# Scaling on ScalarE, two rotary products and three heads turned by VectorE in the second layer of a hybrid encoder

## The chip, the cores and the metric

The kernel runs on one core of one Trainium2 chip. A core has five engines, each with a queue of its own that it works through in order: TensorE (PE in the profile, its weight loads PEld), VectorE (DVE), ScalarE (ACT), GpSimd (POOL) and SyncE (SP), which here only issues DMAs. They meet through semaphores. The metric is the device time of one execution in microseconds (us). Three runs of the kernel before gave 1989.08 us in the median, from 1989.07 to 1989.42.

## What is computed

A trunk of two layers on 256 tokens of width 2048, all in float32. Each layer runs 12 heads of a token mixer and 4 heads of cross-attention into 256 memory tokens, one output projection over all 16 heads, and a squared-ReLU MLP of width 8192. The second layer, the only one that the change touches, is this (cut from the reference):

```
z = n @ b_w_in[j]
q, k, v, qm = split(z, [1536, 2048, 2560])
q = axial_rope(rms_norm(split_heads(q, 12), b_q_norm[j]))
k = axial_rope(rms_norm(split_heads(k, 4),  b_k_norm[j]))
mix = gqa_block_attention(q, k, split_heads(v, 4))
        # per block: s = q k^T * scale; p = softmax(s); p @ v
cross = memory_attention(qm, km, vm)          # 4 heads
h = h + concatenate([mix, cross], -1) @ w_o[i]
# rotary: concatenate([x1*c - x2*s, x2*c + x1*s])
```

## The kernel before

**Products.** A float32 product is made of three fast ones: each operand is split into a rounded high part and the rest. `split` (L506 to L509) does this: ScalarE copies the source into the high part (L508), VectorE subtracts it (L509). Weights come from HBM by DMAs on SP's queue into one of three `raw` buffers (L274), are split in halves of 1024 columns into one of four `hi`/`lo` pairs, and are read by TensorE: twelve matmuls of 512 columns for a half, at L388 (high by high), L391 (high by low weights) and L392 (low by high weights).

**Order.** The Python program runs the halves ("grains") one after the other; each grain is a tick. Other steps are put in at a number of ticks later (`later`). The compiler's scheduler then fixes each engine's order, with this order as priority and a simulated time for readiness. `issue_after(x)` holds back those instructions of a block that run on the same engine as `x`; `past(fn, (a, v))` does so for an ScalarE and a VectorE instruction.

**Attention of the second layer.** The q heads come in three blocks of four (heads 0 to 3, 4 to 7, 8 to 11), each the product of 8 halves. `b_q_done` follows each: `normed_heads` makes the head norms (squares on ScalarE L1614, the root on GpSimd L517, the scaling L1620) and the rotary turn on VectorE: `o = y * cos` (L1600), four products of 32 columns for each head with the sines (L1606, 128x128 in all for each), and the sum (L1608). This is done for two tiles of 128 tokens. The queries are then turned so that a head's features lie on the partitions: block 0 by `queries_far`, block 1 by TensorE (`heads_T`), block 2 by `queries_aside`, where VectorE turns 32x32 blocks (L1582) and eight DMAs on GpSimd's queue (L1585) put them in place. `queries_aside` holds the turn back on VectorE until `box["pT", 5][1]`, the VectorE half of the split of head 5's probabilities.

`attention` gives each head four or three steps. Step 0, `attend`, makes scores on TensorE (L604 to L606), the negated row maximum on VectorE (L562), two exponentials with row sums on ScalarE (L564), the reciprocal of the sums (L567) and two multiplications by it (L569), both on VectorE; the result lies in a buffer `sc`, of which there are three. The last step, `attend3`, multiplies with the values (L698 to L700) and splits the head's output into `cat` (L508, L509), which the output projection reads. Between them the probabilities are turned, in one of two ways:

- three numbers in `steps`, such as `(0, 3, 6)`: `attend2` turns them with four TensorE operations (L616) into PSUM and splits that into `pT`;
- four numbers, such as `(0, 2, 5, 6)`: `turned` lets VectorE turn 32x32 blocks (two instructions, L668) into another of the three `sc` buffers, and four DMAs on SP's queue (L673) put them into the low half of `pT_t`; `halved` splits that in place.

The numbers are ticks after the head's first. Before, the first way is used for heads 4, 5, 6 and 8 to 11, the second for the memory heads and heads 0 to 3 and 7.

**After the last head.** The output projection's first two column blocks run beside all this. Their last chunk of weights, for heads 8 to 11, is handled by `late_products`, and its splits are held back behind certain steps: the first half of the second block behind `box["scaled", 9]`, the last scaling of head 9.

## Time and profile before

| | |
|---|---|
| median of three runs | 1989.08 us |
| the profiled execution, its own time | 1989.6 us |
| its span, first to last instruction | 1987.8 us |
| granted TensorE clock, mean | 0.999 |
| VectorE busy, whole span | 1729.1 us (87%) |
| ScalarE busy, whole span | 1443.7 us (73%) |
| second layer's memory heads, scores to outputs | about 1116 to 1157 us of the span |
| heads 0 to 11, scores to outputs | about 1193 to 1275 us of the span |

The page of the profile gives busy times of engines, the chain of work that ended last, and groups of instructions by line. The timeline gives start, duration, engine, line, operation, what is written from what, shape and count, and in brackets how long the engine stood idle before and for whom. A matmul's record lasts from its first row to the last of its result, so records overlap: what one costs TensorE is the distance from its start to the start of the next.

### The profile page before, as it was taken

The numbers are of one execution on the slowest core, as the hardware profiler recorded it, in microseconds if no ns is written. First come the engines' busy times: TensorE is split into PE (matmuls) and PEld (weight loads), VectorE is DVE, ScalarE is ACT, GpSimd is POOL, SyncE is SP. The second block draws the span as 40 slices with busy tenths as digits, with TensorE's granted clock in tenths as the row PEclk, the third lists the DMA queues.
The fourth block names the chain that finished last, engine by engine and source line by source line (L and its number), as shares of the span: only waits on it lengthen the run. The fifth ranks groups of instructions, "written<-read, shape, count | busy, mean of one in ns | idle before, by whom it ended". The sixth has DMA issues, their size and how long they took to land.

```text
span 1987.8 us, 33096 instructions
## 1 busy us (share of the span) xinstructions
PE 1977.8 (99%) x12816; PEld 1796.3 (90%) x12816; DVE 1729.1 (87%) x2098; ACT 1443.7 (73%) x2109; POOL 152.6 (8%) x205
## 2 busy tenths in 40 slices
PE   9999999999999999999999999999999999999998
PEld 8999999899999999999998888889999999999997
DVE  6777777589999999999999879789999999999997
ACT  6755555478887878777887657668788777877786
POOL 0000000000000000000001001001000000000001
PEclk9999999999999999999999999999999999999999
DMA  7856555768777777777778765668777777777775
GB/s 289 319 193 209 199 193 184 267 210 258 218 231 236 229 230 239 225 241 232 223 228 222 269 221 172 218 205 260 239 225 227 236 230 229 237 229 241 228 227 157
DMA packets 112862, 453.51 MB, mean 228 GB/s; under 512 B 19009, under 2 KB 42689, under 8 KB 65345
## 3 DMA queue, kind: packets, MB, share of 16 engines
q1 hardware_dynamic: 92320, 414.43, 61.1%
q0 software_dynamic: 20096, 36.45, 10.4%
q8 instruction: 100, 1.64, 0.3%
q10 hardware_dynamic: 288, 0.52, 0.1%
q14 instruction: 58, 0.47, 0.1%
HBM read 397.78 MB, written 4.19 MB: 202 GB/s over the span
## 4 chain that ended last, share of the span: by engine, by line
PE 98%; DVE 1%; issue 0%; DMA 0%; ACT 0%; SPq 0%; POOL 0%; DVEq 0%; POOLq 0%; ACTq 0%
PE ps_u L411 35%; PE ps_s L411 10%; PE p L1231 10%; PE p L1235 10%; PE p L1234 10%; PE ps_m L391 7%; PE ps_m L392 7%; PE ps_m L388 7%; DMA raw<-in_w_first 0%; PE sc_ps L605 0%; PE sc_ps L604 0%; PE sc_ps L606 0%; PE av L698 0%; PE av L699 0%; PE av L700 0%
## 5 line engine op out<-in xcount | busy, mean ns | idle before, releaser
L411 PE MATMUL ps_u<-hT,uh 128*128 128x256 f32 x3812 | 662.5, 276 | 0.0
L411 PEld LDWEIGHTS ps_u<-hT,uh 128*128 128x128 f32 x3812 | 578.7, 188 | 5.7
L411 PE MATMUL ps_u<-hT,ul 128*128 128x256 f32 x1964 | 542.6, 276 | 0.0
L508 ACT ACTIVATE uh<-raw_U 128x1024 fp32r<-128x1024 f32 x258 | 273.5, 1061 | 154.0 <-PE ps_u L411 151.6
L411 PEld LDWEIGHTS ps_u<-hT,ul 128*128 128x128 f32 x1964 | 368.7, 188 | 0.0
L508 ACT ACTIVATE hi<-raw 128x1024 fp32r<-128x1024 f32 (+1 forms) x215 | 222.1, 1037 | 183.0 <-PE ps_m L392 93.1
L509 DVE TENSOR_TENSOR lo<-raw,hi 128x1024 fp32r<-128x1024 f32 (+1 forms) x215 | 255.0, 1191 | 108.0 <-ACT hi L508 107.2
L509 DVE TENSOR_TENSOR ul<-raw_U,uh 128x1024 fp32r<-128x1024 f32 x258 | 314.2, 1219 | 9.2 <-ACT uh L508 9.2
L509 DVE TENSOR_TENSOR tl<-t,th 128x2048 fp32r<-128x2048 f32 x120 | 274.8, 2290 | 51.4 <-ACT th L508 51.1
L508 ACT ACTIVATE th<-t 128x2048 fp32r<-128x2048 f32 x120 | 231.0, 1925 | 91.3 <-PE p L1235 91.3
L509 DVE TENSOR_TENSOR bl<-b,bh 128x1536 fp32r<-128x1536 f32 x120 | 210.2, 1752 | 0.0
L1199 POOL DMA_DIRECT2D t<-b x120 | 104.4, 870 | 1156.9 <-ACT t L1198 1097.2
L1231 PE MATMUL p<-th,a_s 128*128 128x512 f32 x480 | 187.5, 391 | 0.0
L1234 PE MATMUL p<-tl,a_s 128*128 128x512 f32 x480 | 187.2, 390 | 0.0
L1235 PE MATMUL p<-th,a_s 128*128 128x512 f32 x480 | 186.7, 389 | 0.0
L508 ACT ACTIVATE bh<-b 128x1536 fp32r<-128x1536 f32 x120 | 178.8, 1490 | 3.5
L411 PE MATMUL ps_s<-nT,hi 128*128 128x256 f32 x896 | 154.6, 277 | 0.0
L1235 PE MATMUL p<-bh,a_s 128*128 128x512 f32 x360 | 140.9, 391 | 0.0
L1234 PE MATMUL p<-bl,a_s 128*128 128x512 f32 x360 | 140.1, 389 | 0.0
L1231 PE MATMUL p<-bh,a_s 128*128 128x512 f32 x360 | 140.1, 389 | 0.0
L411 PEld LDWEIGHTS ps_s<-nT,hi 128*128 128x128 f32 x896 | 135.3, 188 | 0.2
L411 PE MATMUL ps_s<-nT,lo 128*128 128x256 f32 x448 | 124.2, 277 | 0.0
(298 smaller groups left out, 3669.2 us busy)
## 6 DMA issues: line engine op xcount, KB each, us to landing
raw_U<-in_w_up SPq DMA_DIRECT2D x128, 1024.0 KB, 6.4
b<-in_w_pair SPq DMA_DIRECT2D x120, 1024.0 KB, 5.8
raw<-in_w_o SPq DMA_DIRECT2D x32, 1024.0 KB, 5.0
t<-b POOLq DMA_DIRECT2D x120, 256.0 KB, 6.6
raw<-in_w_b SPq DMA_DIRECT2D x21, 1024.0 KB, 5.4
raw<-in_w_av SPq DMA_DIRECT2D x12, 1024.0 KB, 5.0
raw<-in_w_aq SPq DMA_DIRECT2D x12, 1024.0 KB, 4.9
raw<-in_w_ak SPq DMA_DIRECT2D x12, 1024.0 KB, 4.8
```

What stands on the lines that cost most here:

```text
L388: first = nc.tensor.matmul(ps, ah, hi[:, s], start=st, stop=False)
L391: nc.tensor.matmul(ps, ah, lo[:, s], start=False, stop=False)
L392: final = nc.tensor.matmul(ps, al, hi[:, s], start=False, stop=sp)
L411: ins = nc.tensor.matmul(ps, x, acts[:, k, part], start=k == n == 0, stop=k == KT - 1 and n == 2)
L508: first = nc.scalar.activation(dst_hi, src, AF.Copy)
L509: return first, nc.vector.tensor_tensor(dst_lo, src, dst_hi.bitcast(F32), op=ALU.subtract)
L1199: nc.gpsimd.dma_start(s[:, 3, :], b[:, 1, :], accum_op=ALU.add)
L1231: ins = nc.tensor.matmul(ps, a[:, 0, ai, :], hi[:, s], start=entered, stop=False, skip_group_check=True)
L1234: nc.tensor.matmul(ps, a[:, 0, ai, :], lo[:, s], start=False, stop=False, skip_group_check=True)
L1235: nc.tensor.matmul(ps, a[:, 1, ai, :], hi[:, s], start=False, stop=ends, skip_group_check=True)
```

## The change

In the second layer (`box["layer"]` is 1 there) the two multiplications by the reciprocal go to ScalarE, for all 16 heads. The four sine products of the rotary turn become two, each over both halves of a head's features. And heads 4, 5 and 6 take the second way of turning; with head 7 they are now one call of `attention`, with the same first and last ticks as before.

```diff
@@ softmaxed
         for s in range(NT):
-            box["scaled"] = nc.vector.tensor_scalar(sc[:, s, :], sc[:, s, :], rs[:, s : s + 1], None, op0=ALU.mult)
+            if box["layer"]:
+                box["scaled"] = nc.scalar.activation(sc[:, s, :], sc[:, s, :], AF.Copy, scale=rs[:, s : s + 1])
+            else:
+                box["scaled"] = nc.vector.tensor_scalar(sc[:, s, :], sc[:, s, :], rs[:, s : s + 1], None, op0=ALU.mult)
@@ normed_heads, turned_by
-            for a in range(2):
-                for b in range(2):
-                    nc.vector.tensor_tensor(y2v[:, :, a, b, :], yv[:, :, a, 1 - b, :],
-                                            sv[:, None, a, b, :].to_broadcast([P, 4, 32]), op=ALU.mult)
+            for b in range(2):
+                nc.vector.tensor_tensor(y2v[:, :, :, b, :], yv[:, :, :, 1 - b, :],
+                                        sv[:, None, :, b, :].to_broadcast([P, 4, 2, 32]), op=ALU.mult)
@@ b_q_done
             if blk == 1:
-                attention(jobs[:3], 1, 2, (0, 3, 6))
-                attention(jobs[3:], 7, 2, (0, 2, 5, 6))
+                attention(jobs, 1, 2, (0, 2, 5, 6))
```

## The prediction

> **What bounds the kernel now.** I read the page of the profile first: its busy times, the row of granted clock, and the chain that ended last.

> ```profile
> PE 1977.8 (99%) x12816; PEld 1796.3 (90%) x12816; DVE 1729.1 (87%) x2098; ACT 1443.7 (73%) x2109; POOL 152.6 (8%) x205
> ...
> PEclk9999999999999999999999999999999999999999
> ...
> PE 98%; DVE 1%; issue 0%; DMA 0%; ACT 0%; SPq 0%; POOL 0%; DVEq 0%; POOLq 0%; ACTq 0%
> ```

> TensorE is busy for 1977.8 of 1987.8 us at full clock and carries 98% of the chain: only ten microseconds are not its own. So two things can move the time: fewer TensorE instructions, or a new hole between them. Second, the view of busy times by stretch, for the part in which heads 0 to 11 are worked on.

> ```profile
> core 0: us, PE busy (x) PEld busy (x) DVE busy (x) ACT busy (x) POOL busy (x), PEclk, DMA share, GB/s
> 1190.00:1230.00 40.00, 40.00 (x205) 34.23 (x204) 34.46 (x68) 29.46 (x88) 7.03 (x8) 1.00 0.53 181
> 1230.00:1250.00 20.00, 20.00 (x113) 17.30 (x112) 18.88 (x38) 11.91 (x27) 4.48 (x8) 1.00 0.66 201
> 1250.00:1275.00 25.00, 25.00 (x148) 22.02 (x147) 18.38 (x35) 14.65 (x34) 0.00 (x0) 1.00 0.30 95
> ```

> TensorE has no gap in these 85 us. VectorE is next (71.7 us, 84%), and nearly full from 1230 to 1250 (18.88 of 20); ScalarE has 56.0 us (66%), so 29 us to spare. Work of those two is worth nothing by itself, only through what TensorE would come to wait for.

> **The change part by part.** First what leaves TensorE: the turns of heads 4, 5 and 6, four instructions each. The timeline of TensorE at head 6's:

> ```profile
> 1245.12 0.39 PE L391 MATMUL ps_m<-lo,cat 128*128 128x512 f32 x1
> 1245.35 0.60 PE L616 MATMUL pt_a<-ident,sc 128*128 128x128 f32 x4
> 1245.71 0.36 PE L698 MATMUL av<-pT,vb 128*128 128x256 f32 x1
> 1245.91 0.28 PE L699 MATMUL av<-pT,vb 128*128 128x256 f32 x1
> 1246.03 0.28 PE L700 MATMUL av<-pT,vb 128*128 128x256 f32 x1
> ```

> The four take 0.36 us from start to start (1245.35 to 1245.71), and the matmul behind them takes 0.20 us to the next start where its like takes 0.12 (1245.91 to 1246.03): 0.08 more. That is 0.44 us for a head, 3 x 0.44 = **1.3 us** off TensorE. All of it is on the bounding engine, so the bounds are 0 (the freed time is spent waiting for a head) and 1.3 us; I take 1.3, since no row shows TensorE waiting here.

> What comes in for the turn, on three queues, from the timeline at head 2, with the time to landing from the view of the tile `pT_t`:

> ```profile
> 1217.75 1.16 DVE L668 STREAM_TRANSPOSE sc_t<-sc 128x256 f32<-128x256 f32 x2 [1.73 <-DMA pT_t<-sc_t]
> ...
> 1218.94 2.48 SPq L673 DMA_DIRECT2D pT_t<-sc_t  x4
> ...
> DMA to landing us min/median/max: 1.7/2.2/5.0
> ...
> L509 DVE TENSOR_TENSOR pT_t<-pT_t x25: 484/643/696, 116.6 to 1253.8; 128x512 fp32r<-128x512 f32 x13, 128x320 fp32r<-128x320 f32 x12
> ...
> L509 DVE TENSOR_TENSOR pT<-pt_a,pT x7: 665/682/693, 1238.8 to 1271.0; 128x512 fp32r<-128x512 f32 x7
> ```

> For each of three heads: 1.16 us on VectorE, 2.48 us of SP's queue (twelve DMAs in all), 2.2 us to land. The split that follows costs the same either way (643 against 682 ns). VectorE gets 3 x 1.16 = 3.5 us more. From exponentials to a readable `pT_t` a head now takes some 4.5 us longer than by TensorE (1.16 + 1.9 to the last issue + 2.2, less the 0.6 of four transposes): that latency has to be hidden by the ticks between the head's first and last step, which don't move.

> Second, the scaling. On VectorE a pair runs from 1214.21 to the next start at 1214.79; on ScalarE the nearest row is a copy of the same shape with a column as scale, four in a group:

> ```profile
> 1214.21 0.62 DVE L569 TENSOR_SCALAR sc<-sc,rs 128x256 f32<-128x256 f32 x2
> 1214.79 1.23 DVE L509 TENSOR_TENSOR lo<-raw,hi 128x1024 fp32r<-128x1024 f32 x1
> ...
> 410.04 1.72 ACT L538 ACTIVATE hT<-h_t,first 128x256 fp32r<-128x256 f32 x4 [2.13 <-DMA h_t<-h_t]
> ```

> VectorE loses 0.58 to 0.62 us a head; ScalarE gets two at 0.43 = 0.86 us. For the 12 heads of the stretch that is -7.0 us on VectorE and +10.3 us on ScalarE, which then has 66 of 85 us. Before, reciprocal and scaling stood behind each other on VectorE; now ScalarE waits for the reciprocal and VectorE (or TensorE) for the scaling. What stands behind the waiting copy on ScalarE are the weight splits, and TensorE reads those. The view of waits for the stretch 1108 to 1280, and of SP's own queue in it:

> ```profile
> ACT hi L508 <- PE ps_m L392: 23.6, 17, 1.7
> ...
> DVE sc_t L668 <- DMA pT_t<-sc_t: 2.4, 2, 1.7
> ...
> SPq L274 <- DVE lo L509: 83.9, 16, 16.9
> ```

> Seventeen times the split of weights stood still until TensorE gave a buffer back, 23.6 us in all: where that is so, the four buffers are full, and a split that comes a microsecond later is hidden by the three halves (2.7 us each, twelve matmuls at 0.23) ahead of it. I cost the scaling at nothing; if the cover were gone, each head would cost its new hops, bounded by 0 and 0.86 us, 10 us for 12. The row nearest to these ends is the one of full buffers. The twelve new DMAs stand on SP's queue between the loads of weights, 3 x 2.48 = 7.4 us in all. Those loads themselves wait 83.9 us in this stretch for VectorE to free a `raw` buffer, in 16 waits of 5.2 us in the mean; a load held up for 2.48 us lies inside that, so I cost the DMAs at nothing for the weights, and at up to 2.48 us a head if the loads were late already. Behind a turn that waits on VectorE for its buffer (2.4 us in two waits now) stand subtractions of weights, under the same cover. The hold on head 9's scaling now acts on ScalarE's copy of that half and not on VectorE's subtraction: some microseconds later for a half that is not read before head 8's output is there.

> Third, the sine products. Four take 0.81 us (1197.71 to 1198.52); two of 128x256 lie between 0.74 (a pair of `cat` subtractions) and 0.85 us (two that do not overlap):

> ```profile
> 1197.71 0.89 DVE L1606 TENSOR_TENSOR b_y<-b_y,sin_q 128x128 f32<-128x128 f32 x4
> 1198.52 0.16 DVE L567 RECIPROCAL rs<-sm 128x2 f32<-128x2 f32 x1
> ...
> 1243.80 0.74 DVE L509 TENSOR_TENSOR cat<-av,cat 128x256 fp32r<-128x256 f32 x2
> ...
> L1150 DVE TENSOR_TENSOR c<-c x60: 417/425/428, 436.8 to 1917.2; 128x256 f32<-128x256 f32 x60
> ```

> For 8 tiles that is from +0.3 to -0.6 us of VectorE: nothing, and not on TensorE's path.

> The sum on VectorE in the stretch is 3.5 - 7.0 = -3.5 us, on ScalarE +10.3, on TensorE -1.3. Against the profiled execution: 1989.6 - 1.3 = 1988.3; it stands 0.5 us above the median of the runs, so on the median 1989.1 - 1.3 = **1987.8 us**.

> **The rivals.** The place to look is where queries of heads 8 to 11 are made, since `queries_aside` stands on VectorE behind the split of head 5, and that split now comes after DMAs. The rows, from the timelines of VectorE, SP, GpSimd and TensorE:

> ```profile
> 1228.50 1.14 DVE L668 STREAM_TRANSPOSE sc_t<-sc 128x256 f32<-128x256 f32 x2
> 1229.71 2.48 SPq L673 DMA_DIRECT2D pT_t<-sc_t  x4
> 1238.80 1.28 DVE L509 TENSOR_TENSOR pT<-pt_a,pT 128x512 fp32r<-128x512 f32 x2
> 1240.00 2.10 DVE L1582 STREAM_TRANSPOSE b_y_h<-b_o 128x512 f32<-128x512 f32 x2
> 1241.73 4.48 POOL L1585 DMA_DIRECT2D b_y_h<-b_y_h  x8 [18.67 <-ACT cat L508]
> 1252.02 0.68 DVE L509 TENSOR_TENSOR qT<-b_y_h,qT 128x512 fp32r<-128x512 f32 x1
> 1252.89 0.28 PE L604 MATMUL sc_ps<-kT,qT 128*128 128x256 f32 x1
> 1255.05 0.40 PE L388 MATMUL ps_m<-hi,cat 128*128 128x512 f32 x1
> 1257.79 0.38 PE L616 MATMUL pt_a<-ident,sc 128*128 128x128 f32 x2
> ```

> Today the chain is: split of head 5 ends at 1240.08, queries turned, eight DMAs, split until 1252.70, scores of head 8 at 1252.89, without slack. With three `sc` buffers, two hold scores of two heads, so each turn writes where the one before it is still being read by its DMAs (the wait of 1.73 us above is this). A turn then follows the last at 1.16 + 1.9 + 2.2 + hops, about 5.4 us: head 3's at 1228.5, head 4's at 1233.9, head 5's at 1239.3; it has landed at about 1244.6 and is split at 1246.0. That is 5.9 us after today's 1240.08, and the scores of head 8 move to 1258.8.

> *The gain is given back.* The steps of a head's own chain, by the view of groups by line:

> ```profile
> L564 ACT ACTIVATE sc<-sc_ps,nm 128x256 f32<-128x256 f32 x40 | 18.6, 476 | 10.2 <-DVE nm L562 8.3 <-DVE sc_t L668 1.9
> L562 DVE TENSOR_REDUCE nm<-sc_ps 128x2 f32<-128x512 f32 x20 | 13.4, 684 | 2.0 <-PE sc_ps L606 2.0
> L508 ACT ACTIVATE cat<-av 128x256 fp32r<-128x256 f32 x20 | 7.6, 381 | 12.8 <-PE av L700 12.8
> L508 ACT ACTIVATE pT<-pt_a 128x512 fp32r<-128x512 f32 x7 | 4.0, 597 | 2.8 <-PE pt_a L616 2.8
> ```

> TensorE has reached 1257.79 - 1.3 = 1256.5 with work that needs no later head. Head 7's turn, two cadences after head 5's at 1250.1, is split at 1256.8 and its output is in `cat` at 1258.1: holes of about 0.7 us in all. Then come 2.7 us of products with it and 0.72 us of scores for each of heads 8 to 11 (six matmuls at 0.12), until about 1264.4. Head 8's chain from the end of its scores (1259.5) to `cat` takes 0.68 for the maximum, 0.95 for two exponentials, 0.16, 0.86 for the scaling, 0.44 for the turn on TensorE, 0.60 and 0.68 for the split, 0.80 for the values and 0.38, in sum 5.55 us, and eight hops between engines at the 0.19 us seen from 1252.70 to 1252.89: 7.1 us, to 1266.6. That is another 2.2 us. Holes of 2.9 us less 1.3 give +1.6: **1990.7 us**. For it speaks the length of the chain; against it that VectorE is freed of 3.5 us and that the scheduler may place the turn of head 3 earlier.

> *Slower.* TensorE's order is fixed by the scheduler's simulated times. If it puts scores of head 8 ahead of matmuls that could cover, or takes the DMAs for quicker than they are, the whole 5.9 us stand in TensorE's queue: +5.9 - 1.3 = +4.6, **1993.7 us**. It decides as soon as head 5's split ends more than about 4 us after today's time and no matmul of the output projection is queued ahead of the scores. [...]

> *It does nothing.* The heads' outputs come in as fast as the chain lets them, and TensorE's saved 1.3 us are a wait for head 7 or 11: **1989.1 us**. For it speaks that scores of head 8 start 0.19 us after their queries are ready (1252.70); against it that twelve matmuls of other heads lie right behind.

> **How the numbers follow.** Forecast 0.50, with a range of its own from 1986.6 (a further microsecond from the smoother VectorE) to 1988.8; nothing 0.17; given back 0.20; slower 0.11; a gain of over 4 us 0.02, since TensorE has only 1.3 us of this work to lose and its holes outside lie at the kernel's ends. The measurement can tell about 0.2% (4 us) from no change: below 1985.1 is faster (0.02), above 1993.1 slower (0.11), the rest the same (0.87). The range goes from 1986.6 to 1992.0, which takes in the given-back case with 1.3 us to spare and leaves out the slower one.

> **What would show it.** Right, if TensorE stays without a gap from 1190 to 1275, L616 has 16 records in place of 28, and the end of the attention comes 1.3 us earlier. The given-back case shows as idle time of TensorE between 1250 and 1275 with scores of head 8 after 1257; the slower one as one hole of 4 us or more ahead of L604. The sum is wrong if ScalarE's copy waits for the reciprocal long enough that the split of weights no longer waits for TensorE but TensorE for it.

## The result and the profile after

The kernel after takes 1992.27 us in the median of 22 runs (1990.51 to 1994.13), the kernel before 1989.1 us in 22 runs beside them (1988.25 to 1990.79): a ratio of 1.0016, with a 95% interval from 1.0009 to 1.0022. That is 3.2 us slower where 1.3 us faster was forecast, and 0.3 us above the range. A difference this small is within the 0.2% that the prediction took for the least that can be told, but the interval excludes 1: the loss is there, and its place can be seen.

In the kernel after the lines stand a little lower: scaling L570, scores L607 to L609, TensorE's turn L619, VectorE's turn L671 and its DMAs L676, values L701 to L703, the queries' turn L1585 and its DMAs L1588. The page, its busy times and the head of the chain that ended last:

```profile
PE 1977.8 (99%) x12804; PEld 1794.7 (90%) x12804; DVE 1721.9 (87%) x2056; ACT 1453.9 (73%) x2141; POOL 151.0 (8%) x205
...
PE 96%; DVE 1%; DMA 1%; ACT 1%; issue 0%; SPq 0%; DVEq 0%; POOL 0%; POOLq 0%; ACTq 0%
```

Twelve TensorE instructions are gone, VectorE is busy for 7.2 us less and ScalarE for 10.2 us more: the work has moved the way that was foreseen. But the chain has 2% less of TensorE, and DMAs now stand in it. Busy times by stretch show where:

```profile
1190.00:1230.00 40.00, 40.00 (x214) 34.50 (x213) 32.62 (x60) 35.37 (x101) 6.38 (x8) 1.00 0.54 176
1230.00:1250.00 20.00, 18.30 (x87) 14.80 (x86) 17.80 (x27) 11.40 (x24) 4.47 (x8) 1.00 0.62 176
1250.00:1275.00 25.00, 23.21 (x133) 19.63 (x133) 14.16 (x25) 15.90 (x40) 0.00 (x0) 1.00 0.36 127
```

Before, TensorE was busy for all of the 85 us; now it lacks 1.70 and 1.79 us in the second and third stretch, while VectorE has 64.6 us of work there in place of 71.7. No engine is overloaded; TensorE waits for something late. The timeline of TensorE names three waits (in brackets the idle time ahead of the row, and for whom):

```profile
1247.88 0.73 PE L392 MATMUL ps_m<-hi,cat 128*128 128x512 f32 x2 [1.30 <-DVE cat L509]
1249.01 0.50 PE L391 MATMUL ps_m<-lo,cat 128*128 128x512 f32 x1 [0.40 <-DVE lo L509]
...
1254.72 0.39 PE L607 MATMUL sc_ps<-kT,qT 128*128 128x256 f32 x1 [1.79 <-ACT qT L508]
1254.94 0.29 PE L608 MATMUL sc_ps<-kT,qT 128*128 128x256 f32 x1
1255.07 0.28 PE L701 MATMUL av<-pT_t,vb 128*128 128x256 f32 x1
```

They make 3.5 us. Counted from start to start, less the usual distance, they make 4.0 us, and with a fourth, ahead of L702 at 1276.39, 4.3. Besides, the first matmul behind the last two of these holes takes longer to the next start (0.22 us from 1254.72, 0.23 from 1276.39) than its like further on (0.12). The traces also show that the loss lies here: from the first product with `cat` to the first product of the MLP (L411) TensorE takes 104.0 us before (1217.77 to 1321.81) and 107.9 us after (1216.86 to 1324.73), 3.8 us more. With 4.3 us of holes that leaves at most 0.5 us of the 1.3 us that the turns were to free. The two executions reach this stretch 0.9 us apart, the kernel after earlier; why was not followed up.

Who made TensorE wait is seen on the other two engines. ScalarE, where heads 5, 6 and 7 come from their turns at 1241.57, 1247.06 and 1252.05:

```profile
1241.57 0.64 ACT L508 ACTIVATE pT_t<-pT_t 128x512 fp32r<-128x512 f32 x1 [1.40 <-DMA pT_t<-sc_t]
1242.11 1.05 ACT L508 ACTIVATE hi<-raw 128x1024 fp32r<-128x1024 f32 x1
1243.07 0.36 ACT L508 ACTIVATE cat<-av 128x256 fp32r<-128x256 f32 x1
...
1252.05 0.63 ACT L508 ACTIVATE pT_t<-pT_t 128x512 fp32r<-128x512 f32 x1 [3.14 <-DMA pT_t<-sc_t]
1252.59 0.61 ACT L508 ACTIVATE qT<-b_y_h 128x512 fp32r<-128x512 f32 x1
1253.11 1.04 ACT L508 ACTIVATE hi<-raw 128x1024 fp32r<-128x1024 f32 x1
1254.05 0.61 ACT L508 ACTIVATE qT<-b_y_h 128x512 fp32r<-128x512 f32 x1
```

and VectorE behind the split of head 5:

```profile
1241.59 1.18 DVE L671 STREAM_TRANSPOSE sc_t<-sc 128x256 f32<-128x256 f32 x2 [0.96 <-DMA pT_t<-sc_t]
1242.67 0.67 DVE L509 TENSOR_TENSOR pT_t<-pT_t 128x512 fp32r<-128x512 f32 x1
1243.24 2.11 DVE L1585 STREAM_TRANSPOSE b_y_h<-b_o 128x512 f32<-128x512 f32 x2
1245.25 1.13 DVE L671 STREAM_TRANSPOSE sc_t<-sc 128x256 f32<-128x256 f32 x2
1246.28 1.21 DVE L509 TENSOR_TENSOR lo<-raw,hi 128x1024 fp32r<-128x1024 f32 x1
1247.38 0.44 DVE L509 TENSOR_TENSOR cat<-av,cat 128x256 fp32r<-128x256 f32 x1
```

In this trace a step that waits holds up those behind it on its engine. Head 4's output was in PSUM at 1240.1; ScalarE stood until 1241.57 for the DMAs of head 5's turn and made `cat` only at 1243.07; VectorE then had the split of head 5, the queries' turn, head 7's turn and a weight ahead of its half of `cat`, which came at 1247.38, and TensorE's first hole ends 0.5 us later. The rows of VectorE start with a wait of another kind: a turn stood 0.96 us until the DMAs of the one before had read its buffer. At the last hole both splits of queries stand behind head 7's split, which waits 3.14 us for its DMAs; but the last DMA of the queries themselves landed only at 1252.31, so the order can account for a part of that hole at most. The view of waits, from 1190 to 1285, has for this step, in total, times and the longest, first before, then after:

```profile
ACT pT_t L508 <- DMA pT_t<-sc_t: 4.3, 3, 1.9
```

```profile
ACT pT_t L508 <- DMA pT_t<-sc_t: 11.2, 6, 3.1
```

### The profile page after: what moved, and what is told of

The parts are those of the page before. It is cut to its first block, busy times and chain, and to the rows that moved or that the text cites. A ratio compares the mean times of both kernels' runs of the same rounds, so it can differ in the third digit from the quotient of the medians.

```text
span 1990.5 us, 33090 instructions
## 1 busy us (share of the span) xinstructions
PE 1977.8 (99%) x12804; PEld 1794.7 (90%) x12804; DVE 1721.9 (87%) x2056; ACT 1453.9 (73%) x2141; POOL 151.0 (8%) x205
## 4 chain that ended last, share of the span: by engine, by line
PE 96%; DVE 1%; DMA 1%; ACT 1%; issue 0%; SPq 0%; DVEq 0%; POOL 0%; POOLq 0%; ACTq 0%
PE ps_u L411 35%; PE p L1234 10%; PE p L1238 10%; PE p L1237 10%; PE ps_s L411 9%; PE ps_m L391 7%; PE ps_m L388 7%; PE ps_m L392 7%; DMA first<-in_x 0%; DMA pT_t<-sc_t 0%; DVE nT L539 0%; ACT hi L508 0%; PE sc_ps L607 0%; PE sc_ps L609 0%; PE sc_ps L608 0%
## 5 line engine op out<-in xcount | busy, mean ns | idle before, releaser
L411 PE MATMUL ps_u<-hT,uh 128*128 128x256 f32 x3812 | 662.5, 276 | 0.0
L411 PEld LDWEIGHTS ps_u<-hT,uh 128*128 128x128 f32 x3812 | 578.6, 188 | 5.7
L411 PE MATMUL ps_u<-hT,ul 128*128 128x256 f32 x1964 | 542.6, 276 | 0.0
L508 ACT ACTIVATE uh<-raw_U 128x1024 fp32r<-128x1024 f32 x258 | 273.5, 1061 | 152.9 <-PE ps_u L411 150.1
L411 PEld LDWEIGHTS ps_u<-hT,ul 128*128 128x128 f32 x1964 | 368.6, 188 | 0.0
L509 DVE TENSOR_TENSOR lo<-raw,hi 128x1024 fp32r<-128x1024 f32 (+1 forms) x215 | 255.3, 1192 | 110.3 <-ACT hi L508 109.4
L508 ACT ACTIVATE hi<-raw 128x1024 fp32r<-128x1024 f32 (+1 forms) x215 | 222.2, 1039 | 175.0 <-PE ps_m L392 89.1
L509 DVE TENSOR_TENSOR ul<-raw_U,uh 128x1024 fp32r<-128x1024 f32 x258 | 313.9, 1218 | 8.6 <-ACT uh L508 8.6
L509 DVE TENSOR_TENSOR tl<-t,th 128x2048 fp32r<-128x2048 f32 x120 | 274.7, 2289 | 51.0 <-ACT th L508 50.6
L508 ACT ACTIVATE th<-t 128x2048 fp32r<-128x2048 f32 x120 | 230.8, 1923 | 91.5 <-PE p L1238 91.5
L509 DVE TENSOR_TENSOR bl<-b,bh 128x1536 fp32r<-128x1536 f32 x120 | 210.1, 1751 | 0.0
L508 ACT ACTIVATE bh<-b 128x1536 fp32r<-128x1536 f32 x120 | 178.7, 1489 | 3.5
L411 PE MATMUL ps_s<-nT,hi 128*128 128x256 f32 x896 | 154.6, 277 | 0.0
L411 PEld LDWEIGHTS ps_s<-nT,hi 128*128 128x128 f32 x896 | 135.3, 188 | 0.2
L411 PE MATMUL ps_s<-nT,lo 128*128 128x256 f32 x448 | 124.2, 277 | 0.0
```

The lines of the kernel that those rows point to most:

```text
L411: ins = nc.tensor.matmul(ps, x, acts[:, k, part], start=k == n == 0, stop=k == KT - 1 and n == 2)
L508: first = nc.scalar.activation(dst_hi, src, AF.Copy)
L509: return first, nc.vector.tensor_tensor(dst_lo, src, dst_hi.bitcast(F32), op=ALU.subtract)
```

## The experiments

All were measured in five rounds beside the kernel before. There are 22 timed runs of after, 5 of turn_only, turn_two and late_half, 7 of bufs4_late and 11 of each other kernel. "Idle" is the sum of the brackets ahead of TensorE's rows from 1236 to 1268 us in the one profiled run of each; the median is of the timed runs, so the two need not agree to a microsecond. The profiled run of hold4 is the slowest of its eleven (1993.94 us), that of q7 the fastest (1990.84 us). The expectations measure holes from start to start, up to 1280 us, so that the 3.5 us here are 4.3 us there.

| kernel | median us | ratio to before, 95% interval | idle us |
|---|---|---|---|
| after | 1992.27 | 1.0016 [1.0009, 1.0022] | 3.5 |
| scale_only | 1989.37 | 1.0003 [0.9994, 1.0011] | 0 |
| no_turn | 1989.78 | 1.0004 [0.9995, 1.0013] | 0 |
| turn_only | 2000.03 | 1.0056 [1.0043, 1.0068] | 7.1 |
| hold4 | 1991.89 | 1.0012 [1.0003, 1.0021] | 2.8 |
| hold_none | 1992.64 | 1.0017 [1.0009, 1.0026] | 3.1 |
| bufs4 | 1990.34 | 1.0008 [0.9999, 1.0017] | 1.2 |
| bufs4_hold4 | 1991.37 | 1.0010 [1.0001, 1.0018] | 2.4 |
| turn_one | 1988.98 | 1.0001 [0.9992, 1.0010] | 0 |
| turn_two | 1997.00 | 1.0038 [1.0024, 1.0052] | 5.2 |
| bufs4_two | 1992.83 | 1.0017 [1.0008, 1.0026] | 2.8 |
| late_half | 1996.84 | 1.0036 [1.0024, 1.0049] | 5.6 |
| bufs4_late | 1994.80 | 1.0028 [1.0017, 1.0038] | 4.8 |
| no_land | 1988.69 | 0.9999 [0.9991, 1.0008] | 0.4 |
| q7 | 1992.03 | 1.0014 [1.0005, 1.0023] | 2.3 |
| two_q7 | 1992.91 | 1.0018 [1.0009, 1.0027] | 2.3 |
| bufs4_q7 | 1991.12 | 1.0010 [1.0001, 1.0018] | 2.3 |
| hold4_order | 1989.73 | 1.0003 [0.9994, 1.0012] | 1.4 |
| bufs4_hold4_order | 1990.44 | 1.0008 [0.9999, 1.0018] | 0.7 |

### Which part of the change costs time

`scale_only` is before with the scaling on ScalarE alone, `no_turn` is after without the last of its three edits, `turn_only` is before with that edit alone.

```diff
 # no_turn, against after
-                attention(jobs, 1, 2, (0, 2, 5, 6))
+                attention(jobs[:3], 1, 2, (0, 3, 6))
+                attention(jobs[3:], 7, 2, (0, 2, 5, 6))
```

`scale_only`:

> The kernel before with only the second layer's scaling moved to ScalarE. If the turn makes the holes: no hole, 1989.1 us within 0.5. If the scaling makes them: holes of 1 us or more, 1990.5 to 1992 us.

`no_turn`:

> The changed kernel with heads 4 to 6 turned by TensorE again; scaling on ScalarE and two sine products stay. If the turn by VectorE makes the holes: TensorE without a hole in 1190 to 1285 us, 28 records of the turn on TensorE, 1989.1 us within 0.5. If the scaling on ScalarE makes them (its copies hold up the splits behind them): holes of 1 us or more stay, 1990.5 to 1992 us.

`turn_only`:

> The kernel before with heads 4 to 6 turned by VectorE and nothing else of the change. If the turn makes the holes: 4 to 6 us of holes, since VectorE has 7 us more to do here than in the changed kernel, 1992 to 1994 us. If the scaling makes them: no hole, 1987.8 us.

Without the turns there is neither a hole nor a loss that can be told from none: scaling costs 0.5 us in the medians, scaling and rotary products together 0.9, both inside the intervals. The turns alone cost 11 us, far more than the 1992 to 1994 us expected, and beside the other two edits 3.2: those pay only as relief for the queues that the turns fill (which of the two does was not tried apart). So the loss is that of the turns.

In turn_only the waits of ScalarE for landings make 15.0 us, and there are four holes, the last two of them:

```profile
1254.27 0.51 PE L391 MATMUL ps_m<-lo,cat 128*128 128x512 f32 x1 [1.60 <-DVE lo L509]
1262.16 0.58 PE L604 MATMUL sc_ps<-kT,qT 128*128 128x256 f32 x1 [3.28 <-ACT qT L508]
```

### Is it the hold on the queries, or the chain of buffers?

The first two theories. The hold in `queries_aside` passes head 5's delay on to the queries of heads 8 to 11; and three `sc` buffers make each turn wait for the DMAs of the one before. `hold4` holds the queries' turn behind head 4's split, `hold_none` behind nothing, `bufs4` gives a fourth buffer, `bufs4_hold4` both.

```diff
 # hold4
-            with tc.issue_after(box["pT", 5][1].ins):
+            with tc.issue_after(box["pT", 4][1].ins):
 # hold_none
+            with nullcontext():
 # bufs4, in all five places
-... tag="sc", bufs=3 ...
+... tag="sc", bufs=4 ...
```

`hold4`:

> The changed kernel, but the turn of the queries of heads 8 to 11 on VectorE is held back only behind the split of head 4, not of head 5. If that hold is what makes TensorE wait for the scores of head 8: the turn comes at about 1237 and not 1243, the hole of 1.8 us ahead of L607 is gone, and the time falls by about 2 us to 1990.3. If the hole comes from VectorE's load or the chain of DMAs of heads 5 to 7: the hole stays at 1.5 us or more, 1992 us.

`hold_none`:

> The kernel after, three buffers, without any hold on the queries' turn: the scheduler places it by its own estimate. Theory A (the hold passes head 5's delay on to the queries): the queries' turn comes before 1238, the hole ahead of head 8's scores goes, and with it 1.95 of 4.3 us: 1990.0 to 1990.8. Theory B (queues in order): the queries' eight DMAs then lie among those of the turns, a split of queries or of a turned head waits on ScalarE ahead of a cat, and holes of 3 us or more in all stay, elsewhere: 1991.3 to 1993.

`bufs4`:

> The kernel after with a fourth buffer for scores and turns (four places: bufs=3 becomes bufs=4 under the tag of the scores). Theory A (chain of buffers): each of the turns of heads 3 to 7 waits until the DMAs of the turn before have read their buffer, so the turns of heads 5 to 7 and all behind them come late; with a fourth buffer VectorE's turns wait for DMA under 1 us in all (7.8 us now), head 5's split ends 2 to 3 us earlier (by 1241), the 4.3 us of holes on TensorE between 1245 and 1277 fall below 1.0, and the time is 1988.0 to 1989.5. Theory B (landing and queues in order): what stands in the queues of ScalarE and VectorE waits for the landing of a turn's DMAs, 4.5 us after the turn whatever the buffers, and cat and lo of heads 4 and 5 stand behind it; the turns start earlier but the holes stay at 3 us or more in all, and the time is 1991.3 to 1992.8.

`bufs4_hold4`:

> The kernel after with the fourth buffer and with the queries' turn held behind head 4's split only (instead of head 5's). Theory A: buffers and hold together were the delay; queries of heads 8 to 11 are ready before 1249, TensorE has no hole above 0.4 us, 1987.6 to 1988.8, below the kernel before. Theory B: moving the hold only moves the hole, as it did with three buffers (1991.9): 1991 to 1993, with one hole of 2 us or more behind a cat on ScalarE.

The hold alone is not the cause: with hold4 at 1991.9 and hold_none at 1992.6 nothing is won that can be measured. With an earlier queries' turn, in hold4, the hole ahead of head 8's scores goes and one of 2.84 us comes ahead of L388. ScalarE of hold4 around it:

```profile
1248.87 0.63 ACT L508 ACTIVATE qT<-b_y_h 128x512 fp32r<-128x512 f32 x1 [3.06 <-DMA b_y_h<-b_y_h]
1250.62 0.63 ACT L508 ACTIVATE pT_t<-pT_t 128x512 fp32r<-128x512 f32 x1 [1.12 <-DMA pT_t<-sc_t]
1251.15 1.04 ACT L508 ACTIVATE hi<-raw 128x1024 fp32r<-128x1024 f32 x1
1252.10 0.36 ACT L508 ACTIVATE cat<-av 128x256 fp32r<-128x256 f32 x1
```

Now the queries' split waits for its own DMAs, head 6's split for its own, and head 5's `cat`, which TensorE needs, stands behind both. The fourth buffer took back about 2 of the 3.2 us (1990.34 us, between the two expectations), and left a hole of 0.82 us behind another `cat` and one of 0.35 us ahead of TensorE's turn of head 8, which waited for the scaling. With hold and buffer together it was 1991.37, so the two gains don't add up, and the expectation of a kernel below before missed.

### Does the loss grow with the number of heads?

`turn_one` gives only head 6 to VectorE (head 7 was there before), `turn_two` heads 5 and 6; `bufs4_two` is turn_two with four buffers. `late_half` puts the split of a turned head and its values one tick later, `bufs4_late` does so with four buffers.

```diff
 # turn_one
+                attention(jobs[:2], 1, 2, (0, 3, 6))
+                attention(jobs[2:], 5, 2, (0, 2, 5, 6))
 # turn_two
+                attention(jobs[:1], 1, 2, (0, 3, 6))
+                attention(jobs[1:], 3, 2, (0, 2, 5, 6))
 # late_half
+                attention(jobs, 1, 2, (0, 2, 6, 7))
```

`turn_one`:

> The kernel after, with heads 4 and 5 turned by TensorE again, and head 6 by VectorE as in the change (one head of the three, with its steps a tick earlier for head 7 too). Theory A (a chain of turns one behind the other through three buffers): two turns in a row, of heads 6 and 7, leave the chain short, no hole above 0.5 us, 0.4 us below the kernel with none of the three turned (1989.8): 1989.0 to 1989.8. Theory B (each turned head brings its own wait for a landing): a third of the 2.9 us that the three cost against none (1992.7 with 1.3 taken off, against 1989.8): 1990.2 to 1991, with one hole of 0.7 us or more before 1260.

`turn_two`:

> The kernel after with head 4 alone turned by TensorE again; heads 5, 6 and 7 by VectorE, three turns in a row. Theory A (turns queue up behind each other through three buffers, and the delay grows with their number): between one head (1989.0, no hole) and three (1992.3, holes of 4.3 us in all); holes of 0.5 to 2.5 us in all, 1989.3 to 1991. Theory B (a threshold: only head 4's turn, which stands behind those of heads 2 and 3 and ahead of the queries', starts the delay): no hole above 0.4 us, 1988.3 to 1989.2.

`bufs4_two`:

> The kernel after with a fourth buffer and head 4 turned by TensorE: the version that the runs so far point to. Theory A (the delay is that of the third turn in a row and of its buffers): no hole above 0.4 us, 0.4 us below one head (1989.0): 1988.2 to 1989.2, the same as before within what can be measured. Theory B (each landing blocks ScalarE whatever the buffers): a hole of 0.7 us or more ahead of L388, 1989.8 to 1990.6.

`late_half`:

> The kernel after, three buffers, with the split of a turned head and its values one tick later for heads 4 to 7 (steps 0, 2, 6, 7 in place of 0, 2, 5, 6). Theory A (chain of buffers): the turns themselves come no earlier, the queries' turn still stands behind head 5's split, now a tick later, and the hole ahead of head 8's scores grows from 1.95 to 3 us or more: 1993 to 1996. Theory B (steps that wait for a landing block cat and lo in the queues of ScalarE and VectorE): a tick more lets the landing end first, the waits of ScalarE for pT_t fall from 11.2 us to under 4, the two holes ahead of L392 and L391 (1.47 and 0.57 us) go, and the time is 1989.5 to 1991.

`bufs4_late`:

> The kernel after with a fourth buffer and the steps of late_half. Theory A (the chain of buffers is all): the same as the fourth buffer alone or worse, 1990.3 to 1992. Theory B (both: what the fourth buffer left, a hole of 0.98 us ahead of L388 behind head 5's cat, is the queue of ScalarE): that hole goes, no hole above 0.4 us is left before 1270, and the time is 1988.0 to 1989.3, with 12 transposes fewer.

One head costs nothing that can be measured, as the chain of buffers had it, but two cost 7.7 us and three 3.2, which no theory foresaw. A tick more for the landing makes it worse by several microseconds: with three buffers in the direction that the chain of buffers had, though beyond its range (1993 to 1996 us), with four (1994.8) beyond both expectations, and bufs4_two (1992.8), the version that was to be best, is beyond both too. So neither the number of landings nor the chain of buffers alone sets the loss. The buffers have a part in it: a fourth takes 1.9 us off after, 4.2 off turn_two (where the order on ScalarE changes with it) and 2.0 off late_half. ScalarE of turn_two, ahead of its one hole of 5.19 us, gave the third theory:

```profile
1249.99 0.63 ACT L508 ACTIVATE pT_t<-pT_t 128x512 fp32r<-128x512 f32 x1 [3.00 <-DMA pT_t<-sc_t]
1250.53 0.62 ACT L508 ACTIVATE qT<-b_y_h 128x512 fp32r<-128x512 f32 x1
1254.38 0.63 ACT L508 ACTIVATE pT_t<-pT_t 128x512 fp32r<-128x512 f32 x1 [3.23 <-DMA pT_t<-sc_t]
1254.91 1.04 ACT L508 ACTIVATE hi<-raw 128x1024 fp32r<-128x1024 f32 x1
1255.86 0.61 ACT L508 ACTIVATE qT<-b_y_h 128x512 fp32r<-128x512 f32 x1
```

The second split of queries stands behind head 7's split. (The trace names a DMA of weights as what ended this hole; but TensorE's first matmul behind it reads `qT` and starts at 1256.53, 0.06 us after this split ends.) In bufs4_two the second split stands ahead of head 7's, at 1250.87. In turn_one both splits of queries stand ahead of the turned heads', at 1243.38 and 1246.62.

### Landings, and the order behind them

`no_land` leaves out the twelve DMAs of heads 4 to 6 and splits the turned blocks where they lie. `q7`, `two_q7` and `bufs4_q7` are after, turn_two and bufs4 with head 7's split held behind the queries' splits (in the first two TensorE's order stays the same, instruction for instruction; in bufs4_q7 one matmul moves). `hold4_order` and `bufs4_hold4_order` are hold4 and bufs4_hold4 with that hold and with head 6's split held behind head 5's `cat`.

```diff
 # queries_beside
-            split(hi, lo, raw...)
+            box["asked"] = split(hi, lo, raw...)[0]
 # step of q7; in hold4_order also head 6 behind box["cat", 5][0]
+                with tc.issue_after(box["asked"].ins) if box["layer"] and head == 7 else nullcontext():
                     res, box["pT", head] = halved(prev) if len(steps) == 4 else attend2(prev)
 # turned, no_land
+        if not landing:
+            return pT, blocks
```

`no_land`:

> The kernel after without the twelve DMAs that carry the turned probabilities of heads 4, 5 and 6 to their partitions: their splits read the turned blocks where they lie, so these three heads' weights are not the reference's. VectorE's turns, ScalarE's scaling and all else stay. Theory C, and any theory that puts the loss on landings: no hole above 0.4 us, 12 transposes fewer than before, 1987.6 to 1989.0. Rival (VectorE's longer work and its place in the order make the holes): holes of 1.5 us or more in all stay, 1990 to 1992.5.

`two_q7`:

> The kernel with head 4 turned by TensorE (turn_two) and the same swap; TensorE's order is that of turn_two. Theory C: the second split of queries moves from 1255.86 to about 1252.3, the hole ahead of head 8's scores from 5.2 to 1.0 to 1.8 us, the stretch of half clock behind it goes, and the time falls from 1997.0 by 3.5 to 5 us: 1992 to 1993.5. Rival: above 1995.5.

`q7`:

> The kernel after with one pair of steps swapped: the split of head 7's turned probabilities is held behind the splits of the queries of heads 8 to 11; TensorE's order is the same. Theory C (order on ScalarE's queue: the queries have landed and stand behind a step that waits for other DMAs): the second split of queries starts at about 1252 instead of 1254.05, scores of head 8 start by 1253.1 instead of 1254.72, the hole ahead of them falls from 1.95 to under 0.4 us, the holes ahead of L392 and L391 stay, 1990.2 to 1991.0. Rival (both are late together, since all landings share the DMA engines): the hole stays above 1.5 us, 1991.7 to 1993.

`bufs4_q7`:

> The kernel after with the fourth buffer and the same swap, which here also lets head 5's cat pass head 7's split on ScalarE. Theory C: the hole of 0.98 us ahead of L388 goes, no hole above 0.4 us before 1270, and the time is 1988.6 to 1989.8 (1990.3 without the swap). Rival: the queries' second half lands late and the hole comes back ahead of head 8's scores with 0.7 us or more, 1990 to 1991.5.

`hold4_order`:

> The kernel hold4 (queries' turn behind head 4's split, three buffers) with two more holds: head 6's split of turned probabilities stands behind head 5's cat, head 7's behind the queries' split. Theory C (order): in hold4 head 5's cat stood on ScalarE behind a split of queries that waited 3.06 us and a split of head 6 that waited 1.12 us for DMAs; if it passes head 6's split, the hole of 2.8 us ahead of L388 falls by 1.1 to 2.8 us, and the time from 1991.9 to 1988.5 to 1990.8. Rival (the landings come too late for any order): holes of 2.5 us or more in all stay, 1991 to 1993.

`bufs4_hold4_order`:

> The same with four buffers. Theory C: head 5's cat, which stood behind head 6's split (4.76 us of waiting for its DMAs), is made at about 1244 instead of 1249.0, no hole above 0.5 us is left ahead of L388, and with 12 transposes fewer the time is 1987.6 to 1989.2 (1991.4 without the order). Rival: the hole moves on to head 8's scores, 1 us or more, 1990 to 1991.5.

Without the landings the loss is gone (1988.69 us, expected 1987.6 to 1989.0), though VectorE still turns the three heads, so VectorE's work is not the cause. But no_land leaves out more than a wait: SP's queue has twelve DMAs less, no buffer waits until they have read it, and the scheduler gives TensorE another order. It shows that the loss comes with the DMAs, not by which of these effects. And one pair of swapped steps takes 4.1 us off turn_two (1997.0 to 1992.9, expected 1992 to 1993.5; the runs of the two don't overlap, 1994.9 to 1997.7 against 1990.15 to 1994.4). ScalarE and TensorE of two_q7:

```profile
1250.68 0.62 ACT L508 ACTIVATE qT<-b_y_h 128x512 fp32r<-128x512 f32 x1
...
1252.15 0.62 ACT L508 ACTIVATE qT<-b_y_h 128x512 fp32r<-128x512 f32 x1
...
1254.60 0.63 ACT L508 ACTIVATE pT_t<-pT_t 128x512 fp32r<-128x512 f32 x1 [1.83 <-DMA pT_t<-sc_t]
```

```profile
1252.82 0.39 PE L607 MATMUL sc_ps<-kT,qT 128*128 128x256 f32 x1 [1.39 <-ACT qT L508]
```

The queries had landed by then in turn_two as well, since their DMAs were issued up to 1246.7 and none took more than 3.2 us to land: their second split there waits for nothing but its turn on the queue. bufs4_two, which has the same order of these splits, comes out at the same time as two_q7 (1992.83 and 1992.91 us).

In hold4_order, `cat` passes head 6's split and is made at 1248.11 instead of 1252.10; the hole shrinks from 2.84 to 0.70 us, and the median goes from 1991.89 to 1989.73 (expected 1988.5 to 1990.8). This pair is less clean, since the scheduler also moved six matmuls of TensorE:

```profile
1246.62 0.63 ACT L508 ACTIVATE qT<-b_y_h 128x512 fp32r<-128x512 f32 x1 [2.76 <-DMA b_y_h<-b_y_h]
1247.16 1.05 ACT L508 ACTIVATE hi<-raw 128x1024 fp32r<-128x1024 f32 x1
1248.11 0.36 ACT L508 ACTIVATE cat<-av 128x256 fp32r<-128x256 f32 x1
1248.42 0.63 ACT L508 ACTIVATE pT_t<-pT_t 128x512 fp32r<-128x512 f32 x1
```

Where another landing is late too, the swap gains little. In q7 (1992.03, expected 1990.2 to 1991.0) the second split of queries came at 1252.64 instead of 1254.05 and the hole is still 1.21 us, while the holes behind `cat` and `lo` stay. In bufs4_q7 nothing is gained: both splits of queries now wait for their own DMAs (3.10 and 2.43 us). bufs4_hold4_order gets down to one hole of 0.67 us but to no better median (1990.44, expected 1987.6 to 1989.2).

So two conditions act together: a landing that is late, and a step that TensorE needs standing behind it on the same engine's queue. For two heads the second is shown by a swap that leaves TensorE's order as it was (two_q7). For three heads that swap alone gains nothing (q7), while hold4_order, which differs from after in its holds alone, takes 2.5 of the 3.2 us back with all DMAs in place. What makes a landing late was not settled: from issue to landing a DMA of these heads took from 2.1 us to 4.2 us in after, and ScalarE's longest wait for a landing was 3.1 us in after and 4.5 us in turn_only.

The scaling is not free either once the other holes shrink: in bufs4, bufs4_two, no_land, two_q7, bufs4_q7 and hold4_order TensorE's turn of head 8 waits 0.35 to 0.88 us for it. In two_q7 ScalarE does the scaling of heads 8 and 9 from 1258.79, behind the exponentials of both. These kernels with the scaling left on VectorE were not tried.

No kernel here beats before by more than can be measured. The nearest are turn_one (1988.98), hold4_order (1989.73, with 1.4 us of holes left) and no_land, which leaves out a part of the computation; their intervals take in 1. An order without holes for three heads was not found. Why two heads come out worse than three is seen in the order on ScalarE, but why the scheduler orders them so was not followed up.

## Why the prediction was wrong

- **The step that failed**: the cost of the latency of the new turns. It was written as "that latency has to be hidden by the ticks", and 1.3 us of gain were taken "since no row shows TensorE waiting here". The rows of before can't show a wait that the change creates. The runs show that this latency isn't hidden: ScalarE's waits for landings went from 4.3 to 11.2 us, TensorE idles 3.5 us, and the loss goes where the DMAs go (no_land). The latency itself was put at the median landing, 2.2 us; in after the landings of these heads took up to 4.2 us.
- **Given back** was the right rival in kind, its path right in part. Head 5's split was to end 5.9 us late; it ended 3.3 us late (1243.34 against 1240.08), since the scheduler moved head 3's turn to 1220.47 and head 4's to 1229.80 (1233.9 in the text), the possibility that the text named against it. Scores of head 8 came at 1254.72, not 1258.8. Holes were put at 2.9 us in all and late, at head 7's and head 8's outputs; they were 3.5 us, half of them already from 1246 on, at `cat` of head 4 and the weights behind it. The sum has a slip: from 1258.1, 2.7 us of products and four times 0.72 us of scores end at 1263.7, not 1264.4, so its terms give holes of 3.6 us and 1991.4 us, not 1990.7. What the working left out: what stands in the queue *behind* a split that waits for DMAs. It asked this of SP's queue and of the hold on VectorE, not of ScalarE.
- **The cover**: full weight buffers were to hide a late split (23.6 us of waits of `hi` for TensorE; the row is of the stretch from 1120, not 1108, to 1280). For weights they nearly did (0.40 us of idle for `lo`). But `cat` and `qT` have no such buffers, and they made the other 3.1 us.
- **Scaling at nothing**: right by itself (scale_only, 0.5 us inside the interval), but not in the kernels where TensorE waits for it. A pair took 0.89 to 0.93 us on ScalarE in after (0.86 expected). **Rotary products at nothing**: right within what no_turn can tell; a pair took 0.75 to 0.77 us, inside the bounds of 0.74 and 0.85. **SP's twelve DMAs at nothing** for the weights: the waits of after have none of ScalarE for a load of these weights. **12 transposes, 1.3 us**: the count is right (16 records in place of 28); of the gain the traces show at most 0.5 us (104.0 us before and 107.9 after, with 4.3 us of holes), and the medians can't tell it.
- **Slower**, at 1993.7, lay as near in size as given back at 1990.7 (at 1991.4 that is nearer), and its mechanism occurred too, scores of head 8 in TensorE's queue ahead of work that could cover: 1.79 us of hole in after, 5.2 in turn_two. Turning on VectorE costs 11 us in turn_only and, for the one more head of turn_one, nothing that can be measured; what stands behind the landings may decide between them; that was not tried for this pair.
- The chances were wrong with it: 0.50 for a gain of 1.3 us against 0.20 for given back. The case that the text knew in most detail deserved the most.

## What to carry to other kernels

As seen here, a step that gets its data by a DMA holds up its whole engine until the landing (ScalarE for 11.2 us in after, 15.0 in turn_only): before moving work to such a path, list what stands behind the waiting step on that engine and whether TensorE reads it soon. A fresh landing belongs behind everything that is ready; where a scheduler fixes the order, hold the waiting step behind the ready ones by hand, and look at the order again after each edit, since one edit that looks milder (two heads instead of three) can come out worse (1997.00 us against 1992.27). A saving on the bounding engine of 0.1 us an instruction (0.44 us for a head's four) was not worth the latency here, since that did not lie all under other work: in after a head's split starts 5.3 to 6.3 us after its turn on VectorE does (heads 4 to 6, from 1229.80 to 1235.14, 1235.24 to 1241.57 and 1241.59 to 1247.06).

## What the runs showed of the hardware

```profile
1254.40:1257.70 3.30, 3.30 (x9) 2.59 (x10) 1.89 (x3) 0.00 (x0) 1.78 (x4) 0.53 0.84 187
```

behind hold_none's hole of 2.35 us:

```profile
1247.60:1251.40 3.80, 3.43 (x9) 2.65 (x10) 3.80 (x7) 2.18 (x4) 0.00 (x0) 0.55 0.24 52
```

behind turn_two's of 5.19 us:

```profile
1256.50:1262.00 5.50, 5.47 (x25) 5.22 (x26) 3.29 (x6) 1.68 (x7) 0.00 (x0) 0.66 0.01 1
```

and behind after's of 1.79 us, where it stayed whole:

```profile
1254.70:1259.00 4.30, 4.28 (x27) 3.88 (x28) 3.19 (x6) 1.75 (x8) 0.00 (x0) 1.00 0.38 162
```

Behind hold4's hole of 2.84 us the matmuls of 512 columns start 0.43 us apart instead of 0.23:

```profile
1253.10 0.63 PE L388 MATMUL ps_m<-hi,cat 128*128 128x512 f32 x1
1253.53 0.63 PE L391 MATMUL ps_m<-lo,cat 128*128 128x512 f32 x1
1253.96 0.63 PE L388 MATMUL ps_m<-hi,cat 128*128 128x512 f32 x1
```

The fractions are means over their stretches, and the spacing of the matmuls tells where the clock changed. In hold4 those of 256 columns start 0.21 us apart up to 1256.31 and 0.12 from 1256.50 on, in turn_two 0.21 up to 1260.11 and 0.12 from 1260.30 on. A clock of 0.50 up to there is an estimate that gives the means: 0.59 for hold4 from 1252.50 to 1255.70, if it was 1.00 up to 1253.05, and 0.66 for turn_two from 1256.50 to 1262.00.

So in these traces the clock was down behind each hole of 2.35 us or more (behind turn_only's of 3.28 us it was 0.50 from 1262 to 1268, behind late_half's of 3.65 and bufs4_late's of 4.54 us 0.68 and 0.71), behind one of 1.60 us too (turn_only, which has two more holes of 1.0 to 1.2 us in the 11 us before), and not behind one of 1.79 us; what decides between these short ones was not settled. In turn_two the stretch at 0.66 costs an estimated 0.34 x 5.5 = 1.9 us beside the hole itself: there a hole in mid-kernel is dearer than its length.
